# Two chunks that share one FFN by Strassen's products at the end of a streaming encoder layer

## The chip, the core and the metric

The program runs on one core of a Trainium2 chip. Its engines work beside each other, each through its own list of instructions in order: TensorE (PE) multiplies matrices, VectorE (DVE) and ScalarE (ACT) work elementwise on tiles of 128 partitions, GpSimd (POOL) and SyncE (SP) here mostly start DMA transfers. The metric is the device time of one execution in microseconds (us), lower being better.

## The reference

One layer of an encoder over 2048 prompt tokens and 8 x 16 sample tokens, width 1024, FFN width 2816:

```
u = rms_norm(x, norm_mix) @ w_in               # 1024 -> 2564 columns, split among four mixers
x = x + concat(ssd, swa, shortconv, conformer)(u) @ w_out
hf = rms_norm(x, norm_ffn)
x = x + (silu(hf @ w_gate) * (hf @ w_up)) @ w_down
y = rms_norm(x, norm_final)
```

The mixers are a state-space scan in blocks of 64 tokens, attention over a window of 128 keys, a gated convolution over 3 tokens, and a gated convolution over 31 tokens with a layer norm (the conformer). They carry histories from token to token, so the prompt is worked through in order; the final histories and states are outputs too. Everything is float32.

## The kernel before

Activations lie with features on partitions and tokens along the free axis. The 2176 tokens go through in five chunks of 256, 512, 512, 512 (384 of the prompt and the 128 of the sample) and 384 tokens, named c0 to c4 here.

**Products.** Each float32 operand is split into a high part in the matmul's own format (fp32r) and the low part that is left, by one ACT copy and one DVE subtraction (`split`, L177 to L179). `group` (L198) then issues three matmuls for each k-tile of 128: weight high x operand high (L202), weight high x operand low (L203), weight low x operand high (L204), into one PSUM tile `pm`. A projection tile of 1024 inputs so takes 24 matmuls over the chunk's tokens. For each chunk W_in has 21 such tiles, W_out 8, gate and up 22 each, and down (L861) takes 528 matmuls in rounds of 3 or 4 hidden tiles.

**Weights.** `load_w` (L182) starts a DMA of 512 KB on SP into `wr` (3 buffers), copies the high part `wh` on ACT (L192, 2 buffers) and subtracts the low part `wl` on DVE (L164 is the helper `tt`, 2 buffers). These three stand under `high_priority(offset=AHEAD)`, so that the scheduler puts them well ahead of their place in the code. Each weight is loaded and split anew in each chunk.

**A chunk's way.** `proj_in` (L788) makes the W_in tiles, and `after_in` (L368) does what each mixer needs with a tile as it leaves PSUM; the convolutions' inputs go to `raw` tiles (`raw_tiles`, L311, 2 buffers) with their history before them, and `keep_raw` (L345) sends the new histories out by DMA. `mixers` (L747) is a list of generators: attention and scan block by block, the conformer's 31 taps on each of two tiles (`conf_conv`, L363, on DVE, one instruction a tap, into `mix` tiles), and at the end the two norms `end_conf` (L717) and `end_ssd` (L701) and `mix_tile` (L696), which splits the eight results into the operands of W_out. `proj_out` (L799) multiplies them in the order of tiles 4, 5 (short convolution), 2, 3 (attention), 0, 1 (scan), 6, 7 (conformer) and adds x. `norm2` (L825) makes the FFN's operands, `ffn` (L839) returns its 68 units (gate, up and down tiles), `final` (L886) norms and stores.

**The order of the work.** `weave` (L905) puts steps of one list between the units of another. The main loop (from L918) runs, for each chunk c: W_out(c), W_in(c+1), FFN(c). The mixers of c+1 are spread over the first 85% of FFN(c)'s units, so DVE works on them while PE works on the FFN. The order in which instructions stand on each engine is fixed when the program is built. The last four down units of FFN(c3) are put behind W_out(c4). The last chunk has no chunk behind it; its FFN runs alone, at 384 columns a matmul.

## Time and profile before

| | |
|---|---|
| time, median of 3 runs | 2432.99 us (2431.43 to 2434.88) |
| span of the profiled execution | 2430.4 us |
| PE busy | 2386.1 us in 12701 instructions |
| DVE busy | 1648.1 us |
| ACT busy | 919.5 us |
| moved by DMA | 290.78 MB, mean 120 GB/s |

The profiled execution's span of 2430.4 us lies 2.6 us under the median of the runs and 1.0 under the lowest. A row of a profile names a line of the kernel, the engine, the operation, the tile written and the tiles read, and the shape; matmuls on PE overlap, so their rate is read from the distance between two starts, not from the duration of one.

### The profile page before, as it was taken

To read this page: it belongs to the slowest core of one execution; us is meant where nothing else is said; L and a number is where in the kernel's file an instruction comes from. 1 tells how busy PE (TensorE), PEld (TensorE's weight loads), DVE (VectorE), ACT (ScalarE), POOL (GpSimd) and SP (SyncE) were. 2 spreads that over 40 slices of the span, in tenths; PEclk is the share of its full clock that TensorE was granted. 3 is DMA by queue.
4 is the path that set the end of the run, shared out by engine and by line. 5 is a ranking of instruction groups with operands and counts; after the bars stand their busy time and mean duration, and the time that the engine had idled before them with its cause. 6 is when DMAs were issued, how large, how long until landed. Compare 5 with 4: busy or idle time off the path is not lost.

```text
span 2430.4 us, 32788 instructions
## 1 busy us (share of the span) xinstructions
PE 2386.1 (98%) x12701; PEld 2069.4 (85%) x12701; DVE 1648.1 (68%) x2997; ACT 919.5 (38%) x1460; POOL 86.3 (4%) x159
## 2 busy tenths in 40 slices
PE   7999999999999999999999999999999999999998
PEld 7888999888888888877788888889888888999997
DVE  8998998776975546675895455578864545475445
ACT  5544545444333333344333332334332323343332
POOL 1000000000000000001100000000000000000000
PEclk9999999999999999999999999999999999999999
DMA  6433444542222222353422222254322222343332
GB/s 234 135 117 131 158 155 152 199 157 100 90 92 87 87 91 89 137 167 92 135 96 87 87 87 92 91 191 125 112 87 87 90 94 96 133 152 123 131 119 98
DMA packets 106988, 290.78 MB, mean 120 GB/s; under 512 B 10848, under 2 KB 27456, under 8 KB 106832
## 3 DMA queue, kind: packets, MB, share of 16 engines
q1 hardware_dynamic: 102416, 276.34, 34.4%
q0 software_dynamic: 4416, 12.34, 1.6%
q8 instruction: 100, 1.64, 0.3%
q14 instruction: 56, 0.46, 0.1%
HBM read 277.93 MB, written 10.70 MB: 119 GB/s over the span
## 4 chain that ended last, share of the span: by engine, by line
PE 51%; DVE 1%; DMA 1%; issue 0%; ACT 0%; DVEq 0%; ACTq 0%; SPq 0%; POOLq 0%
PE pm L202 16%; PE pm L204 16%; PE pm L203 16%; PE px L231 0%; PE px L213 0%; PE px L640 0%; PE px L622 0%; PE px L650 0%; DMA x<-x 0%; PE px L549 0%; PE px L566 0%; DVE act L167 0%; DMA raw<-gst 0%; PE px L582 0%; DMA y<-x 0%
## 5 line engine op out<-in xcount | busy, mean ns | idle before, releaser
L202 PE MATMUL pm<-act,wh 128*128 128x512 f32 (+2 forms) x2920 | 1056.1, 362 | 3.6 <-ACT act L179 1.4
L204 PE MATMUL pm<-act,wl 128*128 128x512 f32 (+2 forms) x2920 | 1046.5, 358 | 10.8 <-DVE wl L164 10.8
L203 PE MATMUL pm<-act,wh 128*128 128x512 f32 (+2 forms) x2920 | 1045.5, 358 | 0.9 <-DVE act L164 0.9
L192 ACT ACTIVATE wh<-wr 128x1024 fp32r<-128x1024 f32 (+1 forms) x485 | 504.8, 1041 | 1193.8 <-PE pm L203 819.4
L164 DVE TENSOR_TENSOR wl<-wr,wh 128x1024 fp32r<-128x1024 f32 (+1 forms) x485 | 582.5, 1201 | 298.6 <-ACT wh L192 296.7
L204 PEld LDWEIGHTS pm<-act,wl 128*128 128x128 f32 x2920 | 551.8, 189 | 83.6 <-DVE wl L164 13.6
L202 PEld LDWEIGHTS pm<-act,wh 128*128 128x128 f32 x2920 | 551.6, 189 | 79.7 <-ACT wh L192 5.6
L203 PEld LDWEIGHTS pm<-act,wh 128*128 128x128 f32 x2920 | 552.2, 189 | 68.8 <-DVE act L164 1.3
L202 PE MATMUL pm<-h,wh 128*128 128x512 f32 (+2 forms) x880 | 317.7, 362 | 2.0 <-DVE ft L167 1.4
L203 PE MATMUL pm<-h,wh 128*128 128x512 f32 (+2 forms) x880 | 314.3, 357 | 0.0
L204 PE MATMUL pm<-h,wl 128*128 128x512 f32 (+2 forms) x880 | 314.0, 357 | 0.0
L167 DVE SCALAR_TENSOR_TENSOR ft<-ft,pm 128x512 f32<-128x512 f32 (+2 forms) x220 | 132.5, 602 | 166.2 <-PE pm L204 165.3
L164 DVE TENSOR_TENSOR x<-x,pm 128x512 f32<-128x512 f32 (+1 forms) x224 | 137.3, 617 | 134.7 <-PE pm L204 121.2
L167 DVE SCALAR_TENSOR_TENSOR mix<-raw,tabh,mix 128x384 f32<-128x384 f32 (+3 forms) x360 | 199.2, 589 | 1.9
L202 PEld LDWEIGHTS pm<-h,wh 128*128 128x128 f32 x880 | 165.8, 188 | 27.1 <-ACT wh L192 2.7
L203 PEld LDWEIGHTS pm<-h,wh 128*128 128x128 f32 x880 | 165.9, 189 | 20.9 <-issue 0.7
L204 PEld LDWEIGHTS pm<-h,wl 128*128 128x128 f32 x880 | 165.8, 188 | 20.8
L164 DVE TENSOR_TENSOR h<-ft,h 128x512 fp32r<-128x512 f32 (+2 forms) x110 | 66.8, 608 | 0.0
L179 ACT ACTIVATE h<-ft 128x512 fp32r<-128x512 f32 (+2 forms) x110 | 61.1, 555 | 5.3 <-DVE ft L167 4.5
L164 DVE TENSOR_TENSOR ns<-ns,nt 128x512 f32<-128x512 f32 (+2 forms) x91 | 56.9, 625 | 8.9 <-ACT nt L239 7.9
L164 DVE TENSOR_TENSOR act<-act,pm 128x384 f32<-128x384 f32 x56 | 30.9, 552 | 39.6 <-PE pm L204 39.6
L179 ACT ACTIVATE act<-nt 128x512 fp32r<-128x512 f32 (+2 forms) x72 | 40.2, 578 | 45.2 <-DVE nt L167 44.7
(219 smaller groups left out, 1338.6 us busy)
## 6 DMA issues: line engine op xcount, KB each, us to landing
wr<-w_gu SPq DMA_DIRECT2D x220, 512.0 KB, 3.2
wr<-w_in SPq DMA_DIRECT2D x105, 512.0 KB, 3.3
wr<-w_down SPq DMA_DIRECT2D x80, 512.0 KB, 3.4
wr<-w_out SPq DMA_DIRECT2D x40, 512.0 KB, 3.3
wr<-w_down SPq DMA_DIRECT2D x40, 384.0 KB, 3.1
nt<-x SPq DMA_DIRECT2D x48, 256.0 KB, 3.8
x<-x SPq DMA_DIRECT2D x24, 256.0 KB, 5.1
y<-x POOLq DMA_DIRECT2D x24, 256.0 KB, 4.4
```

The costliest lines, as they stand in the source:

```text
L164: return eng.tensor_tensor(out=out, in0=a, in1=b, op=op)
L167: return eng.scalar_tensor_tensor(out=out, in0=a, scalar=s, in1=b, op0=op0, op1=op1)
L179: act.activation(dst[:, 0, :n], src, AF.Copy)
L192: act.activation(hi[:, :n], rv, AF.Copy)
L202: pe.matmul(ps[:, :T], wh, o[:, 0, :T], start=(i == 0), stop=False)
L203: pe.matmul(ps[:, :T], wh, o[:, 1, :T], start=False, stop=False)
L204: mm = pe.matmul(ps[:, :T], wl, o[:, 0, :T], start=False, stop=(i == n - 1))
```

## The change

c0 and c1 go as before. From c2 on the order is another, and c3 and c4 are worked as one block of 896 tokens in the FFN.

- W_in(c3) is made between the first 18 units of FFN(c2), in the order `FIRST`; c3's mixers run up to unit 41 of that FFN, which now has 72 units (`rounds_last`). Then come W_out(c3), units 41 to 43, W_in(c4) merged with units 44 to 48, units 49 to 57, with c4's mixers beside the units from W_in(c4) on, then W_out(c4) and the units 58 to 71.
- x after W_out of c3 and c4 is stored in a DRAM tile `mid`, and the norm's factors are kept in `r2`. `prep` reads `mid` back, scales it, and makes from each pair of k-tiles (i, i + 4) and the two halves of 448 tokens the seven operands of Strassen's scheme, each split into high and low: `11`, `21`, `22`, and four sums `T1` to `T4`.
- Gate and up: two hidden tiles at a time (a quad: 2 halves of the inputs x 2 hidden tiles x 2 halves of the tokens). `quad_w` loads the two tiles' weights, forms four sums and splits seven half-weights; `quad` runs seven products of 12 matmuls over 448 columns instead of eight, into three PSUM tiles, from which ACT copies partial sums between the products. There are 11 quads of gate and 11 of up. The hidden tiles are split and stored in DRAM (`hmem`) by POOL.
- Down: two passes, one for each half of the tokens, all eight output tiles in the eight PSUM banks at once; the operands come back from `hmem`, and `w_down` is read in each pass.
- The split weights of W_in and W_out are kept in DRAM: c0, c1 and c2 each store a third of the 29 tiles (1 MB each, by POOL), and later chunks load high and low together.
- Weight buffers: `w` (high and low in one, 3 buffers) and `fr` (raw, 2 buffers) replace `wr`, `wh` and `wl`.

The core of the diff (the small helpers, `final2`, and the pools' bookkeeping are left out):

```diff
-B = dict(wr=3, wh=2, wl=2, nt=4, b2=4, ut=3, raw=2, mix=4, h=5, ft=1)
+SOON = 120
+B = dict(w=3, fr=2, nt=3, b2=4, ut=3, raw=2, mix=4, act=16, h=5, ft=1)
...
-    def load_w(src, shape, eng=dve):
+    def split_w(raw, n):
+        d = mk(wp, [P, 2, 1024], "w", F32R, bufs=B["w"])
+        act.activation(d[:, 0, :n], raw, AF.Copy)
+        tt(d[:, 1, :n], raw, d[:, 0, :n].bitcast(F32), ALU.subtract)
+        return d
...
+    def load_w(src, shape, key=None, ci=0):
...
-        raw = mk(wp, [P, 1024], "wr", bufs=B["wr"])
-        hi = mk(wp, [P, 1024], "wh", F32R, bufs=B["wh"])
-        lo = mk(wp, [P, 1024], "wl", F32R, bufs=B["wl"])
...
         with tc.high_priority(offset=AHEAD):
-            sync.dma_start(pat(rv), src)
-            act.activation(hi[:, :n], rv, AF.Copy)
-            tt(lo[:, :n], rv, hi[:, :n].bitcast(F32), ALU.subtract, eng)
-        return pat(hi[:, :n]), pat(lo[:, :n])
+            if key in kept:
+                d = mk(wp, [P, 2, 1024], "w", F32R, bufs=B["w"])
+                sync.dma_start(d.bitcast(F32), kept[key])
+            else:
+                raw = mk(wp, [P, 1024], "fr", bufs=B["fr"])
+                sync.dma_start(pat(raw[:, :n]), src)
+                d = split_w(raw[:, :n], n)
+        if key is not None and key not in kept and key % 3 == ci:
+            kept[key] = dp.tile([P, 2, 1024], F32, tag=f"kept{key}", name=f"kept{key}")
+            pool.dma_start(kept[key], d.bitcast(F32))
+        return pat(d[:, 0, :n]), pat(d[:, 1, :n])
...
-    def mixers(c):
+    def mixers(c, early=False):
...
-        if c["i"]:
+        if not early:
             add((short, 1))
...
-        if not c["i"]:
+        if early:
             c["blocks"] = len(st)
             for j, k0, k1 in convs:
                 add((once(lambda j=j, k0=k0, k1=k1: conf_conv(c, j, k0, k1)), 1))
...
+            if m == 0:
+                c["ss"] = mk(np_, [P, TM], "ns", bufs=1)[:, :T]
+            park = c["i"] >= cfg.nfirst
+            x2 = mk(np_, [P, TM], "nt", bufs=B["nt"]) if park else mk(np_, [P, TM], "x2", bufs=8)
             sync.dma_start(x2[:, :T], x[:, m, o:o + T])
-            wh, wl = load_w(w_out[m], [KT, P])
+            wh, wl = load_w(w_out[m], [KT, P], len(W_IN_TILES) + m, c["i"])
...
             tt(x2[:, :T], x2[:, :T], ps[:, :T], ALU.add)
+            if park:
+                pool.dma_start(mid[:, m, o - tail_off:o - tail_off + T], x2[:, :T])
...
+    def stats2(c):
+        o = (c["off"] - tail_off) // P
+        rstd_of(c["ss"], c["T"], D, r2[:, o:o + c["T"] // P])
+        yield
...
-        for ri, n in enumerate(cfg.rounds):
+        for ri, n in enumerate(rounds):
+            end = ri == len(rounds) - 1
...
-                if q == 0:
+                if q == 0 and not (end and lastone):
                     units += pend
                     pend = []
-            pend = [lambda j0=j - n, n=n, m2=m2, f=(ri == len(cfg.rounds) - 1): down(j0, n, m2, f) for m2 in range(4)]
+            pend += [lambda j0=j - n, n=n, m2=m2, f=end: down(j0, n, m2, f) for m2 in range(4)]
...
+    weave(proj_out(c2), (twice(final(c1)), 0, 2), (twice(norm1(c3)), 0, 3))
+    f = ffn(c2)
+    s3 = proj_in(c3, FIRST)
+    units = s3[:3] + merge(s3[3:], f[:18]) + f[18:41]
+    m3 = mixers(c3, True)
+    nb = c3["blocks"]
+    weave(units, (twice(norm2(c2)), 0, 2), (m3[:nb], units.index(s3[8]) + 1, units.index(s3[-1]) + 6),
+          (m3[nb:], units.index(s3[-1]) + 1, len(units) - 1),
+          (twice(norm1_stats(c4)), 20, 35))
+    s4 = proj_in(c4, FIRST)
+    units = proj_out(c3) + f[41:44] + merge(s4, f[44:49]) + f[49:58]
+    m4 = mixers(c4, True)
+    nb = c4["blocks"]
+    weave(units, ([stats2(c3)], 8, 9), (twice(norm1(c4)), 8, 11), (m4[:nb], units.index(s4[8]) + 1, units.index(s4[-1])), (m4[nb:], units.index(s4[-1]) + 1, len(units) - 1))
...
+    def prep():
+        rb = [spread_one(of_blocks(h * N, N)) for h in range(2)]
+        for i in range(4):
+            u = []
+            for k in (i, i + 4):
+                t = g_tile()
+                load_mid(k, t)
+                for h in range(2):
+                    stt(t[:, h], t[:, h], T_("gffn", k), rb[h], ALU.mult, ALU.mult)
+                u.append(t)
+            w = g_tile()
+            b11, b12, b21, b22 = u[0][:, 0], u[0][:, 1], u[1][:, 0], u[1][:, 1]
+            t1, t2 = w[:, 0], w[:, 1]
+            def put(n, src):
+                d = mk(xp if i < 2 else late["xq"], [P, 2, N], "hf", F32R)
+                split(d, src, N)
+                X[n][i] = d
+            put("11", b11)
+            put("21", b21)
+            put("22", b22)
+            tt(t1, b12, b11, ALU.subtract)
+            put("T1", t1)
+            tt(t2, b22, t1, ALU.subtract)
+            put("T2", t2)
+            tt(b12, b22, b12, ALU.subtract)
+            put("T3", b12)
+            tt(t2, b21, t2, ALU.subtract)
+            put("T4", t2)
+            yield
+    def quad_w(j, g):
+        with tc.high_priority(offset=SOON):
+            ra = mk(wp, [P, 1024], "fr", bufs=B["fr"])
+            rb = mk(wp, [P, 1024], "fr", bufs=B["fr"])
+            sync.dma_start(ra.rearrange("p (a b) -> p a b", b=P), w_gu[j, g])
+            sync.dma_start(rb.rearrange("p (a b) -> p a b", b=P), w_gu[j + 1, g])
+            a11, a12, a21, a22 = ra[:, :512], ra[:, 512:], rb[:, :512], rb[:, 512:]
+            s1 = mk(np_, [P, TM], "ft", bufs=B["ft"])[:, :512]
+            da = split_w(ra, 1024)
+            tt(s1, a21, a22, ALU.add)
+            tt(a21, a11, a21, ALU.subtract)
+            tt(a11, s1, a11, ALU.subtract)
+            tt(a12, a12, a11, ALU.subtract)
+            d2 = split_w(ra, 1024)
+            d1 = split_w(s1, 512)
+            dc = split_w(rb, 1024)
...
+    def product(ps, w, xs, first):
+        wh, wl = w
+        n = len(xs)
+        for i, (a, b) in enumerate(xs):
+            pe.matmul(ps[:, :N], wh[:, i], a, start=first and i == 0, stop=False, skip_group_check=True)
+            pe.matmul(ps[:, :N], wh[:, i], b, start=False, stop=False, skip_group_check=True)
+            mm = pe.matmul(ps[:, :N], wl[:, i], a, start=False, stop=(i == n - 1), skip_group_check=True)
+        tail[0] = mm.ins
+    def quad(w):
+        Z, Y, V = (mk(pm, [P, 512], "pm")[:, :N] for _ in range(3))
+        g1, g2 = g_tile(), g_tile()
+        def go(ps, n, first):
+            product(ps, w[n], [(o[:, 0], o[:, 1]) for o in X[XOF[n]]], first)
+        go(Z, 1, True)
+        act.activation(g1[:, 0], Z, AF.Copy)
+        go(Y, 2, True)
+        go(Z, 6, False)
+        act.activation(g1[:, 1], Z, AF.Copy)
+        tt(g1[:, 0], g1[:, 0], Y, ALU.add)
+        go(V, 5, True)
+        act.activation(g2[:, 0], V, AF.Copy)
+        go(Z, 7, False)
+        act.activation(g2[:, 1], Z, AF.Copy)
+        go(V, 3, False)
+        tt(g2[:, 1], g2[:, 1], g2[:, 0], ALU.add)
+        tt(g1[:, 1], g1[:, 1], V, ALU.add)
+        go(Z, 4, False)
+        return g1, g2, Z
...
+    hmem = [dp.tile([P, 2, 2, N], F32, tag=f"hm{j}", name=f"hm{j}") for j in range(cfg.nff)]
+    def gate2(j):
+        g1, g2, Z = quad(quad_w(j, 0))
...
+    def up2(j):
+        g1, g2, Z = quad(quad_w(j, 1))
...
+        stt(t2[:, 1], t2[:, 1], 0.5, g2[:, 1], ALU.mult, ALU.mult)
+        stt(t2[:, 0], t2[:, 0], 0.5, Z, ALU.mult, ALU.mult)
+        for i, t in enumerate((t1, t2)):
+            for h in range(2):
+                d = mk(hp, [P, 2, TM], "h", F32R)[:, :, :N]
+                split(d, t[:, h], N)
+                pool.dma_start(hmem[j + i][:, h], d.bitcast(F32))
+                hs[j + i, h] = d
+    prepared = twice(prep(), 4)
+    weave(proj_out(c4) + f[58:64], ([stats2(c4)], 8, 9), (prepared[:2], 9, 13))
...
+    weave(f[64:], (prepared[2:], 0, 4))
+    units = []
+    for j in range(0, cfg.nff, 2):
+        units += [lambda j=j: gate2(j), lambda j=j: up2(j)]
+    weave(units, (twice(final(c2)), 0, 2))
...
+    def operand(j, h):
+        if j >= cfg.nff - 2:
+            d = hs[j, h]
...
-            side.append(done)
...
+            with tc.high_priority(offset=AHEAD):
+                d = mk(ht, [P, 2, N], "ht", F32R)
+                sync.dma_start(d.bitcast(F32), hmem[j][:, h])
+        return d[:, 0], d[:, 1]
+    def weights(j, mh):
+        with tc.high_priority(offset=AHEAD):
+            raw = mk(wp, [P, 1024], "fr", bufs=B["fr"])
+            sync.dma_start(raw.rearrange("p (a b c) -> p a b c", a=4, b=2), w_down[:, 4 * mh:4 * mh + 4, j:j + 2])
+            d = split_w(raw, 1024)
...
+        acc = [mk(px if m < 4 else pm, [P, 512], "px" if m < 4 else "pm")[:, :N] for m in range(KT)]
+        body, end = (order[:-2], order[-2:]) if h else (order, [])
+        for j in body:
+            ops = [operand(j + i, h) for i in range(2)]
+            for mh in range(2):
+                wh, wl = weights(j, mh)
+                for i in range(4):
+                    product(acc[4 * mh + i], (wh[:, i], wl[:, i]), ops, j == order[0])
+        if not h:
+            for m in range(KT):
+                drain(h, m, acc[m])
...
```

Where the instructions stand, as the built programs have them. First PE in the program before, where the last accumulation ahead of W_out(c4) ends (`pm_3001`, an up tile of FFN(c3)) and W_out(c4)'s first one begins (`pm_3008`; `act_2589` is the short convolution's operand, `act_2946` the first of attention):

```order
L204 MATMUL pm_3001_17927<-act_2472_14597,wl_3000_17923 128x512
L202 MATMUL pm_3008_17965<-act_2589_15353,wh_3006_17960 128x384
L203 MATMUL pm_3008_17965<-act_2589_15353,wh_3006_17960 128x384
L204 MATMUL pm_3008_17965<-act_2589_15353,wl_3007_17961 128x384
L202 MATMUL pm_3008_17965<-act_2590_15356,wh_3006_17960 128x384
L203 MATMUL pm_3008_17965<-act_2590_15356,wh_3006_17960 128x384
L204 MATMUL pm_3008_17965<-act_2590_15356,wl_3007_17961 128x384
L202 MATMUL pm_3008_17965<-act_2946_17596,wh_3006_17960 128x384
L203 MATMUL pm_3008_17965<-act_2946_17596,wh_3006_17960 128x384
```

And the same place in the changed program (`pm_2196`, `pm_2199` and `pm_2203` are W_out(c4)'s first three tiles, `act_2153` and `act_2154` the short convolution's operands, `act_2187` the first of attention, `px_2175` and `px_2184` the spread factors of the mixers' two norms):

```order
L231 MATMUL pm_2203_14908<-act_2153_14616,w_2202_14906 128x384
L232 MATMUL pm_2203_14908<-act_2153_14616,w_2202_14906 128x384
L233 MATMUL pm_2203_14908<-act_2153_14616,w_2202_14906 128x384
L264 MATMUL px_2175_14702<-con_2_85,n8_2164_14654 128x128 x3
L264 MATMUL px_2184_14755<-con_2_85,n8_2172_14686 128x128 x3
L231 MATMUL pm_2203_14908<-act_2154_14619,w_2202_14906 128x384
L232 MATMUL pm_2203_14908<-act_2154_14619,w_2202_14906 128x384
L233 MATMUL pm_2203_14908<-act_2154_14619,w_2202_14906 128x384
L231 MATMUL pm_2196_14842<-act_2187_14767,w_2195_14840 128x384
L231 MATMUL pm_2199_14874<-act_2187_14767,w_2198_14872 128x384
L231 MATMUL pm_2203_14908<-act_2187_14767,w_2202_14906 128x384
L232 MATMUL pm_2196_14842<-act_2187_14767,w_2195_14840 128x384
```

Before, the tiles were made one after the other with no mixer's matmul between; now three are begun on the short convolution's operands alone, and the mixers' norms stand between them. On DVE, the attention's operands before (`act_2946`, `act_2947`), followed by the FFN's own steps (`ft`, `h`, `wl`):

```order
L164 TENSOR_TENSOR act_2935_17524<-xx1_2548_15101,act_2935_17524 128x384
L164 TENSOR_TENSOR act_2946_17596<-q0_2530_14988,act_2946_17596 128x384
L164 TENSOR_TENSOR act_2947_17599<-q1_2535_15021,act_2947_17599 128x384
L167 SCALAR_TENSOR_TENSOR ft_2932_17512<-ft_2932_17512,pm_2939_17533 128x512
L164 TENSOR_TENSOR wl_2950_17604<-wr_2948_17602,wh_2949_17603 128x1024
L164 TENSOR_TENSOR h_2940_17559<-ft_2932_17512,h_2940_17559 128x512
L164 TENSOR_TENSOR wl_2955_17639<-wr_2953_17637,wh_2954_17638 128x1024
```

and in the changed program, where they are `act_2187` and `act_2188`:

```order
L184 SCALAR_TENSOR_TENSOR mix_2132_14423<-ut_2178_14716,mix_2132_14423 128x384
L184 SCALAR_TENSOR_TENSOR xx1_1980_13425<-xx1_1980_13425,tab_1_84,px_2184_14755 128x384
L181 TENSOR_TENSOR act_2177_14711<-mix_2120_14334,act_2177_14711 128x384
L181 TENSOR_TENSOR act_2179_14719<-mix_2132_14423,act_2179_14719 128x384
L181 TENSOR_TENSOR act_2185_14760<-xx0_1975_13386,act_2185_14760 128x384
L181 TENSOR_TENSOR act_2186_14764<-xx1_1980_13425,act_2186_14764 128x384
L181 TENSOR_TENSOR act_2187_14767<-q0_2002_13617,act_2187_14767 128x384
L181 TENSOR_TENSOR act_2188_14770<-q1_2005_13646,act_2188_14770 128x384
L181 TENSOR_TENSOR nt_2194_14838<-nt_2194_14838,pm_2196_14842 128x384
```

Before, FFN steps followed the mixers' last operands; now W_out(c4)'s first addition (`nt_2194`) follows them at once.

More of the change, by code (lines that the diff above doesn't have):

```diff
@@ L225, in rstd_of @@
         stt(r, t, 1.875, r, ALU.add, ALU.mult)
+    def rstd_of(sq, T, n, r=None):
+        nb = T // P
+        v, r_, t = (mk(cp, [P, 8], "n8", bufs=9)[:, :nb] for _ in range(3))
+        r = r_ if r is None else r
+        pc = mk(px, [P, 512], "px")
+        for b in range(nb):
+            pe.matmul(pc[:, b:b + 1], sq[:, b * P:(b + 1) * P], ones[:, 0:1], start=True, stop=True)
+        newton(v, r, t, pc[:, :nb], n)
         return r
@@ new lines, in of_blocks, with spread_one, load_mid @@
+    def of_blocks(o, n_):
+        out, at = [], 0
+        while at < n_:
+            b, t0 = divmod(o + at, P)
+            n = min(P - t0, n_ - at)
+            out.append((r2[:, b:b + 1], t0, at, n))
+            at += n
+        return out
+    def spread_one(r):
+        pr = mk(px, [P, 512], "px")
+        for col, t0, at, n in r:
+            pe.matmul(pr[:, at:at + n], bc(col, [P, P]), ident[:, t0:t0 + n], start=True, stop=True)
+        return pr[:, :N]
+    def load_mid(k, t):
+        sync.dma_start(t, mid[:, k].rearrange("p (h n) -> p h n", h=2))
```

183 lines of the change are left out of this document (130 added, 53 removed).

## The prediction

> **What bounds the kernel now.** I read the page first, then the busy time by stages, then single rows.
>
> ```profile
> span 2430.4 us, 32788 instructions
> PE 2386.1 (98%) x12701; PEld 2069.4 (85%) x12701; DVE 1648.1 (68%) x2997; ACT 919.5 (38%) x1460; POOL 86.3 (4%) x159
> PEclk9999999999999999999999999999999999999999
> ```
>
> TensorE (PE) is busy 98% of the span at full clock, so the number and length of its matmuls set the time, and the other engines matter only where they make it wait. The busy time by stages, one row each, shows where that is:
>
> ```profile
> core 0: us, PE busy (x) PEld busy (x) DVE busy (x) ACT busy (x) POOL busy (x), PEclk, DMA share, GB/s
> ...
> 40.00:360.00 320.00, 318.51 (x2173) 286.85 (x2173) 296.74 (x632) 164.73 (x301) 14.18 (x24) 1.00 0.43 143
> ...
> 1020.00:1200.00 180.00, 169.42 (x739) 137.83 (x738) 130.78 (x251) 66.25 (x99) 22.19 (x33) 0.98 0.48 142
> ...
> 1600.00:1980.00 380.00, 379.11 (x1866) 324.98 (x1865) 247.09 (x409) 137.03 (x216) 17.38 (x31) 1.00 0.35 113
> ...
> 2040.00:2400.00 360.00, 358.65 (x1989) 346.45 (x1988) 195.33 (x279) 119.12 (x158) 4.32 (x8) 1.00 0.39 130
> 2400.00:2430.40 30.40, 18.39 (x103) 17.43 (x101) 18.61 (x40) 6.96 (x13) 0.00 (x0) 0.84 0.18 65
> ```
>
> Three things stand there. The last chunk's FFN (2040 to 2400) runs on PE without a gap while VectorE (DVE) is half idle: that is the work the change shortens. The projection of the sample chunk (1020 to 1200) leaves PE idle for 10.6 us. And while the mixers run (1600 to 1980) DVE works 65% of the time, beside an FFN that covers it.
>
> The time of one matmul is the distance between two starts, since the listed durations overlap:
>
> ```profile
> start us, us, engine line op out<-in xcount [idle before <-releaser]
> ...
> 999.65 0.39 PE L202 MATMUL pm<-h,wh 128*128 128x512 f32 x1
> 999.88 0.39 PE L203 MATMUL pm<-h,wh 128*128 128x512 f32 x1
> ...
> 1000.56 0.39 PE L203 MATMUL pm<-h,wh 128*128 128x512 f32 x1
> ...
> 2198.72 0.33 PE L202 MATMUL pm<-h,wh 128*128 128x384 f32 x1
> 2198.89 0.33 PE L203 MATMUL pm<-h,wh 128*128 128x384 f32 x1
> ...
> 2199.76 0.33 PE L202 MATMUL pm<-act,wh 128*128 128x384 f32 x1
> ```
>
> From 999.65 to 1000.56 are four steps: 227 ns for 512 columns. From 2198.72 to 2199.76 are six: 173 ns for 384. No matmul of 448 columns runs before; halfway between the two is 200 ns, and I take it, because 448 is halfway between the widths.
>
> **The change part by part.**
>
> *Strassen, the gain.* Before, chunks 3 and 4 take 1056 gate and up matmuls and 528 down matmuls each: 1584 x (0.227 + 0.173) = 633.6 us. After, 22 quads of 7 products of 12 matmuls are 1848, and down is 1056, all of 448 columns: 2904 x 0.200 = 580.8 us. The difference is -52.8 us, all on the path, since PE is the bound there. It is the 264 matmuls saved; merging the chunks alone saves nothing. The Trainium skill ("TensorE: Matmul & The Clock Gate", "Wait — 56ns, not 53.3ns?") gives N/2.4 + 2.5 ns, an estimate of 189 ns for 448 columns and of -50 us for the 264; the rows above, 11 ns longer at both widths, decide.
>
> *The sample chunk's wait.* Its first projection ran alone on PE before. These are PE's waits from 1020 to 1200 and DVE's from 1100 to 1200, and PE's stretch just behind the last of them:
>
> ```profile
> PE pm L204 <- DVE wl L164: 10.3, 6, 3.7
> ```
>
> ```profile
> DVE raw L315 <- DMA o_xc_s<-raw: 12.6, 3, 4.8
> DVE raw L171 <- DMA raw<-gst: 5.4, 2, 3.5
> ```
>
> ```profile
> 1161.00:1164.00 3.00, 3.00 (x8) 2.34 (x8) 3.00 (x8) 0.00 (x0) 0.00 (x0) 0.50 0.23 22
> ```
>
> DVE stood on two `raw` buffers that DMAs had not let go, the low part of the next weight (`wl`) queued behind it on DVE, and PE waited 10.3 us for that. In the change all of this chunk's W_in tiles come from DRAM already split (each of the chunks before kept a third), so no `wl` stands behind `raw`, and 18 units of chunk 2's FFN lie between the tiles. I take -10 us, with 0 (the wait only moves to the tiles' readers) and -14 (the stretch at half clock goes too) as ends.
>
> *Chunk 4's mixers before W_out(4), the largest cost.* Before, they were done by 85% of chunk 3's FFN. Now they begin beside W_in(4), and the FFN left beside them is nine units. I count from the last W_in tile (a0's accumulation) on. PE then has 144 matmuls of 512 columns, 66 of 384 (18 of them W_out on the two short-convolution tiles) and a few small ones until it needs the attention's two tiles: 144 x 0.227 + 66 x 0.173 + 3 = 47.1 us. DVE's durations, from the chunk before's mixers:
>
> ```profile
> L164 DVE TENSOR_TENSOR wl<-wr,wh 128x1024 fp32r<-128x1024 f32 x70 | 85.6, 1224 | 47.8 <-ACT wh L192 47.7
> L167 DVE SCALAR_TENSOR_TENSOR mix<-raw,tabh,mix 128x384 f32<-128x384 f32 x60 | 34.9, 613 | 0.6
> ...
> ```
>
> ```profile
> 1754.56 2.73 DVE L167 SCALAR_TENSOR_TENSOR mix<-raw,tabh,mix 128x384 f32<-128x384 f32 x5
> 1757.21 0.68 DVE L167 SCALAR_TENSOR_TENSOR ft<-ft,pm 128x512 f32<-128x512 f32 x1
> 1757.81 1.22 DVE L164 TENSOR_TENSOR wl<-wr,wh 128x1024 fp32r<-128x1024 f32 x1
> 1758.94 0.69 DVE L164 TENSOR_TENSOR b<-b,xC 128x512 f32<-128x512 f32 x1
> 1759.54 0.69 DVE L164 TENSOR_TENSOR h<-ft,h 128x512 fp32r<-128x512 f32 x1
> 1760.15 2.21 DVE L167 SCALAR_TENSOR_TENSOR mix<-raw,tabh,mix 128x384 f32<-128x384 f32 x4
> ```
>
> Starts again: five taps, of 613 ns each by duration, take 2.73, so a tap is (2.73 - 0.61) / 4 = 0.53 us; a weight's low part 1.13; an addition over 512 columns 0.60. In the new order DVE has, up to the sum `ut` of the two convolutions, 60 taps (31.8 us), five low parts of 1024 and four of 256 (5.7 + 1.3), ten additions into x2 (6.0), four 512-wide FFN steps (2.5) and fifteen others, nine over 384 columns (5 us): 52.8 us. Behind `ut` come the two norms (22 tiny steps at some 0.2 us) and fifteen full ones at 0.5 to 0.6, 13 us. So the attention's tiles stand at 65.9 us, and PE, with 47.1 us of work, waits 18.8. The chain between the engines (mean on PE, square on ACT, spread on PE) adds an estimated 1.5, and a wait this long ends in a stretch at half clock like the one above, which costs 1.5. I take +21 us; the ends are 12 (DVE's steps a tenth shorter, 59.3 - 47.1, and no chain or half clock on top) and 28 (a tenth longer, 72.5 - 47.1, and both on top). The Trainium skill (same page, "Why this matters for your kernels") warns of PE gaps of over some 3 us, after which the clock is halved; the row with 0.50 agrees, and by the page this wait would cost about as much as I added.
>
> *Entry to the quads.* `prep` must read x back from DRAM, scale it and make seven operands of each of four pairs of k-tiles. From the spreading of the norm to the first quad PE has 216 matmuls of 512 columns, 49.6 us. DVE in that stretch has 28 low parts, 12 differences and 4 plain ones over 448 (44 x 0.53), 16 scalings (0.60), eleven low parts of weights (3 x 1.13, 4 x 0.87, 4 x 0.60), and 18 FFN and x2 steps (0.60), two more for the first quad's weights: 54.4 us to the first quad's weights, and 66.2 to its last ones, which PE wants at 59.2. So +5 to +7, and the reloads over three `g` buffers, 3.2 us each by the row below, show in part: +9, ends 4 and 15.
>
> ```profile
> wr<-w_gu SPq DMA_DIRECT2D x220, 512.0 KB, 3.2
> ```
>
> *Inside the quads.* A quad is 84 x 0.200 = 16.8 us on PE. DVE has 3.5 low parts of 1024 (4.0), four sums of weights (2.4), three sums of products (1.6) and the gate's or up's steps (2.1 to 4.3): 10 to 12.5 us. It fits, so +2, ends 0 and 25 (a rival).
>
> *Smaller terms.* Chunk 3's mixers share DVE with more FFN than before: 5 us for blocks that wait (0 to 9). From the last quad to down, four operands must be split first: +3 (1 to 6). Storing split weights (30 MB by GpSimd's queue) and reloading lies beside PE work at 120 GB/s of traffic: 0, and if the cover were gone a 1 MB load is some 6 us. Two `fr` buffers in place of three `wr`: +2 (-2 to 25, a rival). The tail stays as it was.
>
> Sum: 2430.4 - 52.8 - 10 + 21 + 9 + 2 + 5 + 3 + 2 = 2409.6 us against the profiled execution. The median of the runs shown, 2432.99, is 2.6 above its span; 2409.6 + 2.6 = 2412 us.
>
> **The rivals.**
>
> *More of the gain stays.* DVE is busy 68% overall and could be ahead at both boundaries; then W_out(4) costs 12 and the entry 4, and the half-clock stretch goes too: 2430.4 + 2.6 - 52.8 - 14 + 12 + 4 + 5 = 2387 us. Against it: DVE cannot begin the 60 taps before their tile is there, and they are half of its sum.
>
> *Slower: two raw buffers starve the first chunk.* The weight loads of chunk 0's 256-token FFN, seen by the low parts in one stretch, and what a load goes through:
>
> ```profile
> 240.00:360.00 120.00, 79.28 (x279) 53.32 (x279) 43.32 (x36) 1.00 0.46 153
> ...
> ```
>
> ```profile
> L192 ACT ACTIVATE wh<-wr 128x1024 fp32r<-128x1024 f32 (+1 forms) x485 | 504.8, 1041 | 1193.8 <-PE pm L203 819.4
> ```
>
> 36 weights in 120 us, one each 3.33 us. A raw buffer is taken for the DMA (3.2), the high part (1.04) and the low part (1.22): 5.5 us, so two give one each 2.75 us. It decides from 6.7 us a cycle on, 1.2 us of queueing on a DVE that is 93% busy in that stage. At 8 us the weights come each 4.0 us, and some 75 of them lose 0.67: +50, 2412 - 2 + 50 = 2460 us. For it: DVE's load there. Against it: w has three buffers, so a late load has a whole weight of slack, and chunk 1 takes a third of its projection's weights already split.
>
> *The quads run at the pace of their chain.* Z passes from PE to ACT and back between products, with three `fr`, `w` and `g` hand-overs a quad. If each quad loses 1.1 us, 22 of them lose 25: 2412 - 2 + 25 = 2435 us, no change that can be told. For it: 12.5 of 16.8 us on DVE in strict order. Against it: a copy of 448 columns is covered by the product between (12 x 0.200 = 2.4 us).
>
> That the change doesn't do what it says is out: in the program's order the 1848 and 1056 matmuls of 448 columns stand there.
>
> **How the numbers follow.** Chances: the forecast 0.60, more of the gain 0.20, quads at their chain's pace 0.09, two raw buffers 0.11. The forecast's own range is 2399 to 2425: its terms' ends lie some 7, 8, 6 and 5 us from the values taken, which as independent errors make 13. The range takes in the first rival, with 3 us for a pitch of 199 instead of 200 ns on 2904 matmuls, and the quads' rival: 2384 to 2436. A measurement of this kernel can tell about 0.2% (4.9 us) from no change: below 2428 is faster. Faster 0.83 (the first two, and a third of the quads' case, where a quad loses less), the same 0.05 (most of what is left of that case), slower 0.12 (the raw buffers, and the quads' bad end).
>
> **What would show it.** Right: matmuls of 448 columns starting 200 ns apart; PE waiting some 17 us before W_out(4), first for the convolutions' sum and then for the attention's tiles, and 5 to 10 us around the first quad; no wait for `raw` in chunk 3. Wrong: PE waiting in small pieces all over chunk 0 for low parts, or in each quad for `w`, or a pitch other than 200 ns.

## The result, and the profile after

The changed kernel takes 2468.18 us (2461.09 to 2471.18, 4 runs) against 2432.64 for the kernel before on the same chip: 1.0136 times as long, 95% interval 1.0116 to 1.0155. It is slower where faster was forecast. The profiled execution has a span of 2459.3 us, 28.9 more than before. It is the fastest of the four, 7 us under their median; what follows accounts for this one.

The page of the changed kernel, its span, the engines and the clock by slices:

```profile
span 2459.3 us, 32394 instructions
PE 2367.5 (96%) x12443; PEld 2052.3 (83%) x12443; DVE 1589.3 (65%) x2997; ACT 876.7 (36%) x1461; POOL 130.8 (5%) x240
...
PEclk9999999999999999999999999999889999999998
DMA  7657445576422222466443136643533323338663
```

PE has 258 matmuls fewer, but is busy only 96% of a longer span, and the clock now falls below full in the slices around 1700 to 1850 us. A longer span with less work means waits. PE's waits, by what it waited for (total, times, longest):

```profile
PE pm L231 <- DVE x L181: 15.0, 7, 9.2
PE px L257 <- DVE ns L181: 12.9, 2, 10.8
PE px L264 <- DVE n L184: 9.3, 3, 4.4
PE pm L231 <- DMA w<-kept: 7.0, 7, 2.0
PE pm L231 <- ACT act L196: 6.9, 3, 3.0
PE pm L233 <- DVE w L181: 5.1, 8, 0.8
PE pm L231 <- ACT hf L196: 4.5, 2, 4.3
```

The second line is the lead-in, which the kernel before has too. To see where the time went I counted the projection and FFN matmuls (PE's `pm` ones and, in the down passes, those into `px`), whose order is the same in both kernels up to the end of W_out(c2), and compared when the same one starts; the column of excess is the stretch less N/2.4 + 13.3 ns for each of them (N columns; a line through the means of the kernel before, 119.9, 173.4 and 227.1 ns at 256, 384 and 512) and less the mixers' small matmuls.

| stretch | before | after | excess before | excess after |
|---|---|---|---|---|
| to the 600th (W_in(c0) and four tiles of W_in(c1)) | 117.2 us | 135.3 us | 15 | 34 |
| to the 2784th (FFN(c0) done) | 460.5 | 477.5 | 11 | 10 |
| to the 5256th (W_out(c2) done) | 1058.9 | 1084.7 | 8 | 17 |
| from there to the last matmul | 1363.4 long | 1366.1 long | 32 | 78 |

So 25.8 us are lost in chunks 0 to 2, which the forecast had at +2; and from there on the 52.8 us gained are spent on 46 us more excess and 10 us more in the mixers' small matmuls, which the forecast had at +30 together.

The first stretch, 17 to 117 us, one row each of before and after (busy time and count of PE first, then the other engines, clock, DMA share, GB/s):

```profile
17.00:117.00 100.00, 98.65 (x698) 89.56 (x699) 93.08 (x219) 58.89 (x115) 5.85 (x10) 1.00 0.51 173
```

```profile
17.00:117.00 100.00, 85.22 (x607) 78.01 (x607) 76.50 (x180) 52.17 (x107) 8.47 (x17) 0.98 0.72 255
```

In the same 100 us PE gets 91 matmuls fewer through, DVE and ACT idle more too, and the DMA traffic is half as high again. The DMA issues of that stretch, first the weight loads before, then loads and stores after (KB each, us to landing), and what ACT waited for there after:

```profile
wr<-w_in SPq DMA_DIRECT2D x24, 512.0 KB, 3.3
```

```profile
fr<-w_in SPq DMA_DIRECT2D x21, 512.0 KB, 4.4
kept<-w POOLq DMA_DIRECT2D x7, 1024.0 KB, 6.4
```

```profile
ACT w L201 <- DMA fr<-w_in: 18.9, 9, 4.1
```

A weight lands 4.4 us after its issue, not 3.3 as before, and ACT waits 18.9 us for weights; before, no wait of ACT for a weight's load stands on its list there.

Chunk 4's wait came, with about the size that was forecast. The stretches around it and around the first quad:

```profile
1696.00:1712.00 16.00, 6.75 (x19) 4.69 (x19) 16.00 (x29) 3.17 (x4) 0.00 (x0) 0.68 0.30 99
1724.00:1744.00 20.00, 15.48 (x68) 13.99 (x67) 11.80 (x40) 5.53 (x12) 0.06 (x1) 0.66 0.13 53
1832.00:1844.00 12.00, 6.18 (x15) 4.32 (x15) 11.36 (x20) 3.99 (x8) 0.00 (x0) 0.61 0.25 84
1853.00:2222.00 369.00, 368.17 (x1827) 341.38 (x1826) 253.15 (x361) 164.47 (x249) 32.68 (x48) 1.00 0.35 118
2230.00:2430.00 200.00, 200.00 (x1002) 187.42 (x1001) 62.80 (x65) 49.33 (x53) 2.44 (x4) 1.00 0.68 223
```

In the first row DVE is busy for all of the 16 us and PE for 6.75, with the clock down at 0.68. The last two rows are the quads and the down passes: PE is busy throughout. Strassen's part does what it was built for.

### The profile page after: what moved, and what is told of

Same layout as the page of the kernel before. It is cut to its first block, busy times and chain, and to the rows that moved or that the text cites. A ratio compares the mean times of both kernels' runs of the same rounds, so it can differ in the third digit from the quotient of the medians.

```text
span 2459.3 us, 32394 instructions
## 1 busy us (share of the span) xinstructions
PE 2367.5 (96%) x12443; PEld 2052.3 (83%) x12443; DVE 1589.3 (65%) x2997; ACT 876.7 (36%) x1461; POOL 130.8 (5%) x240
## 4 chain that ended last, share of the span: by engine, by line
PE 44%; issue 6%; DVE 3%; DMA 2%; ACT 0%; POOL 0%; DVEq 0%; SPq 0%; POOLq 0%; ACTq 0%
PE pm L1102 6%; PE pm L1103 6%; PE pm L1104 6%; PE pm L231 6%; PE pm L232 6%; PE pm L233 6%; PE px L1103 1%; PE px L1102 1%; PE px L1104 1%; DMA nt<-x 1%; DVE w L181 1%; DVE x L184 0%; DMA o_xc_s<-raw 0%; DMA act<-kc 0%; PE px L655 0%
## 5 line engine op out<-in xcount | busy, mean ns | idle before, releaser
L231 PE MATMUL pm<-act,w 128*128 128x512 f32 (+2 forms) x2216 | 804.2, 364 | 16.6 <-DMA w<-kept 7.0
L233 PE MATMUL pm<-act,w 128*128 128x512 f32 (+2 forms) x2216 | 796.8, 360 | 5.2 <-DVE w L181 5.1
L232 PE MATMUL pm<-act,w 128*128 128x512 f32 (+2 forms) x2216 | 795.8, 359 | 1.4 <-DVE act L181 1.4
L201 ACT ACTIVATE w<-fr 128x1024 fp32r<-128x1024 f32 (+3 forms) x375 | 388.3, 1036 | 892.9 <-PE pm L233 524.1
L181 DVE TENSOR_TENSOR w<-fr,w 128x1024 fp32r<-128x1024 f32 (+3 forms) x375 | 448.4, 1196 | 288.3 <-ACT w L201 287.0
L231 PEld LDWEIGHTS pm<-act,w 128*128 128x128 f32 x2216 | 420.2, 190 | 85.2 <-issue 9.4
L233 PEld LDWEIGHTS pm<-act,w 128*128 128x128 f32 x2216 | 420.3, 190 | 64.6 <-DVE w L181 7.5
L232 PEld LDWEIGHTS pm<-act,w 128*128 128x128 f32 x2216 | 420.6, 190 | 59.4 <-DVE act L181 2.3
L1102 PE MATMUL pm<-hf,w 128*128 128x448 f32 x616 | 225.6, 366 | 0.8 <-ACT g L1116 0.6
L1103 PE MATMUL pm<-hf,w 128*128 128x448 f32 x616 | 224.8, 365 | 0.0
L1104 PE MATMUL pm<-hf,w 128*128 128x448 f32 x616 | 223.8, 363 | 0.0
L231 PE MATMUL pm<-h,w 128*128 128x512 f32 (+1 forms) x528 | 192.3, 365 | 19.6 <-DVE x L181 12.9
L232 PE MATMUL pm<-h,w 128*128 128x512 f32 (+1 forms) x528 | 189.2, 359 | 0.0
L233 PE MATMUL pm<-h,w 128*128 128x512 f32 (+1 forms) x528 | 188.3, 357 | 0.0
L181 DVE TENSOR_TENSOR x<-x,pm 128x512 f32<-128x512 f32 (+2 forms) x184 | 107.6, 600 | 67.4 <-PE pm L233 55.1
L231 PEld LDWEIGHTS pm<-h,w 128*128 128x128 f32 x528 | 100.3, 190 | 41.1 <-issue 12.3
L184 DVE SCALAR_TENSOR_TENSOR ft<-ft,pm 128x512 f32<-128x512 f32 (+1 forms) x132 | 78.7, 596 | 84.2 <-PE pm L233 67.2
L1102 PEld LDWEIGHTS pm<-hf,w 128*128 128x128 f32 x616 | 115.6, 188 | 10.6 <-ACT g L1116 1.0
L1104 PEld LDWEIGHTS pm<-hf,w 128*128 128x128 f32 x616 | 115.7, 188 | 9.4
L1103 PEld LDWEIGHTS pm<-hf,w 128*128 128x128 f32 x616 | 115.7, 188 | 8.2
L233 PEld LDWEIGHTS pm<-h,w 128*128 128x128 f32 x528 | 100.4, 190 | 15.2
```

The costliest lines, as they stand in the source:

```text
L181: return eng.tensor_tensor(out=out, in0=a, in1=b, op=op)
L184: return eng.scalar_tensor_tensor(out=out, in0=a, scalar=s, in1=b, op0=op0, op1=op1)
L201: act.activation(d[:, 0, :n], raw, AF.Copy)
L231: pe.matmul(ps[:, :T], wh, o[:, 0, :T], start=(i == 0), stop=False)
L232: pe.matmul(ps[:, :T], wh, o[:, 1, :T], start=False, stop=False)
L233: mm = pe.matmul(ps[:, :T], wl, o[:, 0, :T], start=False, stop=(i == n - 1))
```

## The experiments

Each was run against the kernel before on the same chip; "excess" is as above. Where a row tells of a matmul by its number, it is the count above.

**What slows the first chunks: the stores or the buffers.** Theory A is the traffic of the 1 MB stores, theory B, the forecast's rival, the two raw buffers. The first run stores nothing, the second stores later, the third is the kernel before with two raw buffers.

```diff
-        if key is not None and key not in kept and key % 3 == ci:
+        if False:
```

> The changed kernel with no split weights kept in DRAM: every chunk loads and splits W_in and W_out anew, all else as in the changed kernel. Theory A (the 1 MB stores of split weights are what slows the first chunk's projection: they share the DMA engines with the weight loads): the 600th projection matmul starts within 4 us of the kernel before (117 us) instead of 18 us later, and the whole falls to 2440 to 2455 us, since W_in of the later chunks is split on VectorE again. Theory B (two raw weight buffers are what slows it): the 600th starts at 131 us or later, and the whole stays at 2462 us or more.

```diff
-        if key is not None and key not in kept and key % 3 == ci:
+        if key is not None and key not in kept and ci in (1, 2) and key % 2 == ci - 1:
```

> The changed kernel, but the first chunk keeps no split weights; the second and the third chunk keep one half each, so that chunks 3 and 4 still load all of them split. Theory A (stores): the first stage's 18 us go, the stage around the second chunk's projection loses up to 4 us more, whole 2446 to 2456 us. Theory B (two raw buffers): the first stage stays 14 us or more behind the kernel before, whole 2462 us or more.

```diff
-B = dict(wr=3, wh=2, wl=2, ...
+B = dict(wr=2, wh=2, wl=2, ...
```

> The kernel before with two instead of three raw weight buffers, nothing else. Theory A (stores are the cause in the first chunk): within 5 us of the kernel before, 2433 to 2438 us. Theory B (two raw buffers are the cause): the 600th projection matmul starts 12 us or more later than 117 us, whole 2447 us or more.

Measured: 2452.4 us without stores (ratio 1.0064, 1.0044 to 1.0084), 2458.5 with later stores (1.0102, 1.0082 to 1.0121), 2448.2 for the kernel before with two raw buffers (1.0044, 1.0029 to 1.0059). The 600th matmul starts at 121.8, 121.0 and 122.2 us (before 117.2, changed 135.3). The rows of the stretch without stores and of the kernel before with two raw buffers:

```profile
17.00:117.00 100.00, 95.14 (x680) 85.55 (x679) 88.95 (x209) 58.24 (x116) 4.42 (x10) 1.00 0.53 173
```

```profile
17.00:117.00 100.00, 95.44 (x677) 86.42 (x677) 89.98 (x210) 57.86 (x115) 3.87 (x10) 1.00 0.51 167
```

They are alike: two raw buffers alone cost 5 us here, and the stores the other 14. Neither theory is the whole, but A has three quarters. Three figures lie outside what was expected: the 600th matmul of the first run by 0.6 us, the whole of the second by 2.5, and the whole of the third, which stands where theory B had it. In the kernel before, two raw buffers cost more than this stretch shows: 10 us by the 5256th matmul, and 12 in the median of the whole. Up to the 5256th matmul the run without stores is 5.5 us behind the kernel before, the changed kernel 25.8. The difference of 20 holds the stores and also the reloads in chunks 1 and 2, where PE waits 4 us for `w<-kept`. The kept weights are worth something later: without them the second half of the profiled execution is 16 us longer, probably because W_in and W_out of chunks 3 and 4 are split on DVE again. By the medians, which differ by 16 us and not by the 4 of the profiled executions, it would be some 5 us, if the first half gains the same 20 in them. Storing later (the second run) saves half of the 25.8: the 5256th starts at 1072.8.

**Traffic alone.** To see whether a store hurts by its traffic or by holding one of the three `w` buffers, the same 1 MB is written from a constant tile, after a small copy that waits for the split weight. No chunk loads kept weights here.

```diff
-            pool.dma_start(kept[key], d.bitcast(F32))
+            dm = dp.tile([P, 4, 512], F32, tag=f"kept{key}", name=f"kept{key}")
+            one = mk(cp, [P, 8], "n8", bufs=9)
+            pool.tensor_copy(one[:, :1], d[:, 1, :1].bitcast(F32))
+            pool.dma_start(dm, cn[:, :512].unsqueeze(1).to_broadcast([P, 4, 512]))
```

> The changed kernel, but at each place where split weights are stored the same 1 MB is written from a constant tile instead, started when the split weight is ready, and no chunk loads kept weights. So the traffic is there and no weight buffer is held by a store. Theory A (traffic): the 600th projection matmul starts at 130 us or later, as in the changed kernel (135). Theory B (a store holds one of three weight buffers for its 6 us): it starts at 125 us or earlier, as with no stores (122).

Measured: the 600th starts at 160.1 us, later still than in the changed kernel.

```profile
17.00:117.00 100.00, 73.94 (x512) 68.08 (x512) 62.04 (x142) 43.10 (x82) 15.41 (x26) 0.93 0.89 329
```

```profile
kept<-con POOLq DMA_DIRECT2D x15, 1024.0 KB, 9.4
fr<-w_in SPq DMA_DIRECT2D x19, 512.0 KB, 6.1
```

Weights land after 6.1 us here. But the test is much stronger than wanted. The store itself has no tie to the small copy, and GpSimd issues six in a row right behind the first copy, where the second copy comes only at 50.42 us:

```profile
14.68 4.40 POOL L224 DMA_DIRECT2D kept<-con  x6
```

So 15 stores lie in the stretch where the changed kernel has 7, and each takes 9.4 us, not 6.4. That shows that traffic alone, at twice the stores, delays the loads; it does not show that the real stores' traffic makes up the 14 us, nor that holding the buffer adds nothing.

**More cover for chunk 4's mixers.** Cover is PE work beside which the mixers' work on DVE is hidden.

```diff
-    units = s3[:3] + merge(s3[3:], f[:18]) + f[18:41]
+    units = s3[:3] + merge(s3[3:], f[:18]) + f[18:36]
...
-    units = proj_out(c3) + f[41:44] + merge(s4, f[44:49]) + f[49:58]
+    units = proj_out(c3) + f[36:39] + merge(s4, f[39:44]) + f[44:58]
```

> The changed kernel with five FFN units of the third chunk moved from beside chunk 3's mixers to beside chunk 4's mixers (27 us of TensorE work). If the wait ahead of the last W_out (some 23 us with the half clock) is VectorE being 19 us behind TensorE: it falls to under 5 us, whole 2443 to 2450 us. Rival (the wait only moves to chunk 3's W_out, or it is a DMA that is late): whole 2460 us or more.

Measured: 2463.97 us (1.0118, 1.0103 to 1.0133), 4 less than the changed kernel. The excess from the end of W_in(4) to the end of W_out(4) falls from 23 to 9 us, so DVE's lateness made most of it, though less fell away than was expected (to under 5 us); but chunk 3's stretch has 11 us more, most of it here:

```profile
PE px L655 <- ACT b L644: 7.3, 1, 7.3
```

That is a block of chunk 3's attention that PE reached before its softmax was done. The rival holds, in the whole too: cover taken from one chunk's mixers is missed at the other's.

**What Strassen itself brings.** Each quad with eight plain products; the operands `T1` to `T4` and the sums of weights are not made.

```diff
-        go(Z, 1, True)
-        go(Y, 2, True)
-        go(Z, 6, False)
...
+        def go(ps, t, h):
+            for q in range(2):
+                product(ps, w[t][q], [(o[:, 0], o[:, 1]) for o in X[f"{q + 1}{h + 1}"]], q == 0)
```

> The changed kernel with eight plain products in place of Strassen's seven in each quad: the operands are only the four blocks (16 split tiles in place of 28, no sums), a quad is 96 matmuls of 448 columns, all else as in the changed kernel. Theory A (Strassen gives its matmuls nearly whole, and costs only at the entry): the stretch from the first 448-column matmul to the last of the quads is 53 us longer, the wait ahead of the first quad falls from 17 to under 8 us, whole 2498 to 2515 us. Theory B (the quads wait for VectorE and ScalarE and give the gain back): the quads' stretch is less than 40 us longer, whole under 2490 us.

Measured: 2508.8 us (1.0301, 1.0275 to 1.0327), 41 more than with seven products. From the first to the last matmul of 448 columns it takes 642.2 us against 590.3: 51.9, forecast 52.8. The excess ahead of the first quad falls from 17.3 to 6.4. Theory A holds: the products give their whole gain in the quads, and pay 11 us at the entry.

**Why 512 columns take 229 ns.** In the middle chunks matmuls of the changed kernel start 229.1 ns apart, those of before 227.1 (means over 5029 and 6603). Two runs of the kernel before, one with both parts of a weight in one tile, one with the operands' pools allocated from the other end of the memory (`side="right"` on `ap`, `hp` and `np_`):

```diff
-        hi = mk(wp, [P, 1024], "wh", F32R, bufs=B["wh"])
-        lo = mk(wp, [P, 1024], "wl", F32R, bufs=B["wl"])
+        d = mk(wp, [P, 2, 1024], "w", F32R, bufs=B["wh"])
+        hi, lo = d[:, 0], d[:, 1]
```

> The kernel before, with the high and low part of a weight in one tile of 8 KB a partition, two buffers, instead of two tiles of 4 KB. The 512-column matmuls of the changed kernel start 229 ns apart in the middle chunks, those of the kernel before 227. If the combined weight tile is the cause, it is 229 ns here and the whole some 8 to 12 us over the kernel before; if not, 227 ns and no change.

> The kernel before, with the pools of the operands, hidden tiles and norms allocated from the other end of the on-chip memory, as in the changed kernel. If the place of the operands is the cause of the longer distance between matmuls, it is 229 ns here and the whole some 8 to 12 us over the kernel before; if not, 227 ns and no change.

Measured: 2438.1 us and 227.1 ns with one tile, that is nothing; 2474.7 us (one run) and 233.3 ns with the pools at the other end, 37 us more for a mere change of place. An estimate from the distances in the table at the end, times the matmuls of each width, gives 39. Steps of that run:

```profile
900.00 0.39 PE L203 MATMUL pm<-act,wh 128*128 128x512 f32 x1
900.23 0.40 PE L204 MATMUL pm<-act,wl 128*128 128x512 f32 x1
900.46 0.39 PE L202 MATMUL pm<-act,wh 128*128 128x512 f32 x1
900.70 0.40 PE L203 MATMUL pm<-act,wh 128*128 128x512 f32 x1
900.93 0.39 PE L204 MATMUL pm<-act,wl 128*128 128x512 f32 x1
901.16 0.40 PE L202 MATMUL pm<-act,wh 128*128 128x512 f32 x1
```

Five steps in 1.16 us, where five of before take 1.135. Then the kernel before with unused tiles that move everything, or the operands alone:

```diff
+    pad = mk(cp, [P, 56], "pad")
     tb = mk(cp, [P, NTAB], "tab")
```

> The kernel before with one unused tile of 224 bytes a partition ahead of all others, so that the operands and weights of every projection matmul start at multiples of 256 bytes instead of 32 bytes past one. Theory (the start addresses set the distance between matmuls, as the two layouts with 227 and 233 ns suggest): the distance at 512 columns changes by 2 ns or more, and the whole by 12 us or more, either way. Rival (only the place of operands against weights counts, which is the same as before): 227 ns and 2433 to 2440 us.

```diff
+    pad2 = sp.tile([P, 32], F32, tag="pad2", name="pad2")
     ap = ctx.enter_context(tc.tile_pool(name="ap", bufs=16))
```

> As the run before it, with the operands another 128 bytes on: weights at multiples of 256 bytes, operands 128 past one. Theory (addresses against 64 bytes count): as the run before it. Rival (operands against weights counts): a distance other than in the run before it by 2 ns or more at 512 columns.

Measured: 2435.6 us and 227.1 ns (0.9997, 0.9988 to 1.0006) with everything moved to a multiple of 256 bytes; 2472.2 us (one run) and 232.5 ns with the operands another 128 bytes on. So the shared address made no difference in the places tried, the operand's place against the weight's did, as the rivals in both expectations had it.

**Putting it together.** First, only chunk 3 stores split weights (for chunk 4), and five units go from beside W_in(3) to chunk 4's mixers:

```diff
-        if key is not None and key not in kept and key % 3 == ci:
+        if key is not None and key not in kept and ci == 3:
...
-    units = s3[:3] + merge(s3[3:], f[:18]) + f[18:41]
+    units = s3[:3] + merge(s3[3:], f[:13]) + f[13:36]
```

> The changed kernel, but only chunk 3 keeps split weights (for chunk 4 alone), and five FFN units of the third chunk go from beside W_in(3) (13 instead of 18 there) to beside chunk 4's mixers; chunk 3's own mixers have as many units as in the changed kernel. If the stores are what slows the first three chunks, the second projection's end stands within 7 us of the kernel before (1065 us instead of 1085); if chunk 4's mixers only lack cover, the wait ahead of the last W_out falls from 23 to under 10 us; chunk 3's projection may wait 5 to 12 us more for its raw tiles. Together 2430 to 2446 us. Rival (the waits ahead of W_out(3) and W_out(4) are one budget of cover, and only move): 2448 us or more.

Measured: 2446.55 us (1.0032, 1.0018 to 1.0046). The 5256th matmul starts at 1063.9, chunk 4's excess is 8, and chunk 3's stretch rises from 22 to 38: two parts as forecast, the third dearer; the whole lies between the forecast's range and the rival's. Then the same with two unused tiles of 32 bytes, which put operands and weights at the same place against 256 bytes:

> The kernel of the run with stores by chunk 3 only, with two unused tiles of 32 bytes, so that operands and weights start at multiples of 64 bytes (192 past a multiple of 256). If addresses against 64 bytes set the distance: under 227 ns at 512 columns and under 200 at 448, whole under 2436 us. If only operands against weights counts: 227 and 200 ns as in the kernel before, whole 2434 to 2440 us. If neither: 229 ns, 2446 us.

Measured: 227.1 ns at 512 columns but 202.9 at 448 (changed kernel 200.9 and, for a third of them, 202.6), 2447.83 us (1.0048, 1.0032 to 1.0065), no different from the run without the tiles. The distance at 512 is what "only operands against weights" had, the one at 448 and the whole are not. What is won at 512 columns (2.0 ns each, some 10 us, an estimate from the means) is lost again at 448 (1.5 ns, 4 us) and 256 (2.7 ns, 6 us). In its projection of chunk 3 DVE stands like this:

```profile
1073.04 0.16 DVE L189 SCALAR_TENSOR_TENSOR n<-n,n 128x4 f32<-128x4 f32 x1
1078.72 0.17 DVE L353 COPY raw<-hx 128x3 f32<-128x3 f32 x1 [5.52 <-DMA o_xc_s<-raw]
1078.80 0.15 DVE L186 TENSOR_TENSOR n<-n,n 128x4 f32<-128x4 f32 x1
```

The copy into `raw` waits 5.5 us for the DMA that still reads the tile, and the steps of the norm (`n`) for chunk 2's FFN stand on DVE behind it. PE's waits there:

```profile
PE px L528 <- ACT ut L519: 6.2, 1, 6.2
PE px L269 <- DVE n L189: 5.5, 1, 5.5
```

Four tiles that use `raw` were made in a row; so another order, in which only the last two still follow each other:

```diff
-    s3 = proj_in(c3, FIRST)
+    s3 = proj_in(c3, ("k", "v", "q0", "B", "q1", "C", "dt", "x0", "x1") + FIRST[9:])
```

> The kernel of the run before (stores by chunk 3 only, tiles at 64 bytes), with the first nine W_in tiles of chunk 3 in another order: three that need no raw tile come first, and the four that need one are parted by others. If the two raw tiles are what VectorE waits for there, with the norm's steps behind it: PE's two waits of 5.7 and 6.3 us in the projection of chunk 3 fall to under 2 us each, whole 2430 to 2440 us. Rival (VectorE is simply behind there, whatever it waits for): both stay within 2 us, whole 2445 us or more.

Measured: 2426.93 us (0.9964, 0.9952 to 0.9976), below the range forecast. In that projection PE now waits for one thing:

```profile
PE pm L238 <- DVE w L186: 2.2, 1, 2.2
```

Last, two units moved from chunk 3's mixers to the entry:

```diff
-    units = s3[:3] + merge(s3[3:], f[:13]) + f[13:36]
+    units = s3[:3] + merge(s3[3:], f[:13]) + f[13:34]
...
-    weave(proj_out(c4) + f[58:64], ([stats2(c4)], 8, 9), (prepared[:2], 9, 13))
+    weave(proj_out(c4) + f[56:64], ([stats2(c4)], 8, 9), (prepared[:2], 9, 13))
```

> As the run before, and two FFN units of the third chunk (11 us of TensorE work) moved from beside chunk 3's mixers to behind W_out(4), ahead of the first quad. If chunk 3's mixers have cover to spare and the entry lacks it: the wait ahead of the first quad falls from 17 to 8 us or less with none in its place, whole 6 to 10 us under the run before, 2422 to 2434 us. Rival (it is one budget and only moves): within 3 us of the run before.

Measured: 2424.42 us (0.9953, 0.9941 to 0.9966), within 3 us of the run before. The excess ahead of the first quad falls only from 19.0 to 13.5, and chunk 3's rises from 20.7 to 25.4: the rival holds, it is one budget. The page of this version:

```profile
span 2422.6 us, 32577 instructions
PE 2358.4 (97%) x12443; PEld 2052.6 (85%) x12443; DVE 1656.9 (68%) x3056; ACT 932.7 (38%) x1520; POOL 130.4 (5%) x242
```

By the two ratios it beats the kernel before by 0.5% and the changed one by 1.8%.

## Why the prediction was wrong

Its sum, term by term, in us:

| term | forecast | measured | shown by |
|---|---|---|---|
| Strassen's products | -52.8 | -51.9 | seven against eight products |
| storing and reloading split weights, chunks 0 to 2 | 0 | +20 | no stores: 5256th matmul at 1064.4 for 1084.7 |
| two raw buffers | +2 | +5 | no stores: 5.5 us still behind there (the new places of the tiles are in it) |
| chunk 3's projection | -10 | -3 | excess 11.5 for 14.2 |
| chunk 3's mixers | +5 | +9 | excess and small matmuls |
| chunk 4's mixers ahead of W_out(4) | +21 | +22 | 19 of excess, the rest small matmuls; cover moved: falls by 14 |
| W_out(4)'s own waits | 0 | +4 | excess of its last 174 matmuls |
| entry to the quads | +9 | +16 | eight products: falls by 11 |
| inside the quads | +2 | +5 | 202 ns a matmul |
| last quad to down | +3 | 0 | the first down matmul starts 0.4 us after the last of the quads |
| the tail | 0 | +3 | 18.3 us from the last down matmul to the end, 14.8 before |

*The step that failed* is the one of the smaller terms: "Storing split weights (30 MB by GpSimd's queue) and reloading lies beside PE work at 120 GB/s of traffic: 0". The runs show +20 in its place. The mean over the span was the wrong row. In the stretch where the first stores lie the traffic before was 173 GB/s and a weight's load 3.3 us long; with two raw buffers and no stores ACT already waits 11.5 us for loads there, and with stores, where the load takes 4.4 us, 18.9. The profiled execution's span missed the forecast by 50 us (2459.3 for 2409.6), and this term is 20 of them, the largest but not the whole: the entry and chunk 3's projection are 7 each, and 2 to 4 each come from most of the others. Without the stores the kernel still takes 2452 us, outside the range.

The forecast's rival named the first chunk and its raw buffers and gave it 0.11, but placed the loss in chunk 0's FFN and put it down to queueing on DVE. The excess did not grow in that FFN (10 for 11); it grew in W_in ahead of it, where DVE idled for a quarter of the time and ACT waited for the DMA. The sign given for it, PE waiting in small pieces for low parts, came (`w L181` in the list of PE's waits: 8 times, 5.1 us), but is the smaller part.

*Chunk 3's projection* failed as a place: the wait for `raw` was seen, but it did not go, as the forecast's signs had it: DVE waits 12.3 us for `raw<-gst` in that chunk and 4.2 for `o_xc_s<-raw`. The claim that none of this chunk's low parts stands behind it was right, but other work does. The norm of chunk 2's FFN now stands there (4.4 us at one place), and the order `FIRST` makes four tiles with `raw` in a row. With the tiles parted the profiled execution is 14.4 us shorter, 12.0 of it excess and 2.8 small matmuls in this stretch: the waits and the half clock behind them. The medians differ by 21; the runs of the version without it reach from 2440 to 2450, so the rest is not told apart.

*The entry* was right in kind and short in size: DVE's sum against PE's gave +5 to +7, and it was 16. PE's waits from 1780 to 1853 add up to 10.3 us; the rest is in stretches at a lower clock (0.61 in the row of 1832 to 1844). The reloads over three `g` buffers, which the forecast named, show as a wait of DVE of only 0.6 us. What in the chain set the 16 is shown only as far as the run with eight products goes: 11 of the 16 fall away with the sums and their splits.

*Chunk 4's wait* was forecast to within some 2 us, from the order of the instructions and the durations of before (the steps listed up to `ut` add up to 52.3 us, not 52.8, which changes nothing). Its place was right in part only. PE was to wait first for the convolutions' sum; the longest wait, 9.2 us up to about 1707, came earlier, at a down unit whose PSUM tile was free only when DVE, in its order, got to the addition behind the taps:

```profile
1701.27 4.86 DVE L184 SCALAR_TENSOR_TENSOR mix<-raw,tabh,mix 128x384 f32<-128x384 f32 x9
1706.03 0.69 DVE L181 TENSOR_TENSOR x<-x,pm 128x512 f32<-128x512 f32 x1
```

*The pitch*, the distance between two starts, was forecast at 200 ns for 448 columns; it is 200.9 or 202.6 by where the operands lie. That the pitch of the other widths would change was not in the sum: 512 columns lose 2.0 ns each and 256 win 2.8, some +10 and -6 us by an estimate from the means, spread over the rows of the table. The Trainium skill ("TensorE: Matmul & The Clock Gate", "Wait — 56ns, not 53.3ns?") gives N/2.4 + 2.5 ns, an estimate of 189 ns for 448 columns; no layout here came near, the shortest mean step at 512 columns being 227 ns where it gives 216.

What stays open: how much of the stores' cost is the buffer they hold; what sets chunk 3's remaining excess of some 20 us, which is spread over many blocks; and what makes the other three runs of the changed kernel 5 to 10 us longer than the profiled one.

## What to carry to other kernels

Price a new transfer in the stretch where it will run, by the landing time of the loads it runs beside and the buffers that hide them, not by the mean traffic. A product that saves matmuls is only half the change: count what must be ready before its first one, and whose cover that takes; when two late stages share one cover, moving it between them gains little, and removing a wait (here by the order of four tiles) gains more. And when pools are moved, compare the distance between matmuls before anything else.

## What the runs showed of the hardware

In these runs the distance between two matmuls goes with where the moving operand lies against the stationary one, modulo 256 bytes in a partition (addresses from the built programs, the same for all matmuls of a width unless noted):

| operand's start less weight's | 256 columns | 384 | 448 | 512 |
|---|---|---|---|---|
| 0 (kernel before, the same moved by 224 bytes, and the version at multiples of 64 bytes) | 119.9 ns | 173.4 | 202.9 | 227.1 |
| 64 (changed kernel) | 117.1 | 173.3 | 200.9 | 229.1 |
| 128 (operands another 128 bytes on) | 118.9 | 176.0 | | 232.5 |
| 192 (pools at the other end) | 115.3 | 176.5 | | 233.3 |

At 512 columns the best and the worst differ by 2.7%, at 256 by 4% the other way. Only four differences were tried, with weights loaded for every matmul. At 448 columns the stage counts as well: in the changed kernel a third of these matmuls, all in the quads, have a difference of 0 and start 202.6 ns apart; those at 64 start 201.8 ns apart in the quads and 200.0 in the down passes, which makes the 200.9. Why the place counts was not looked into.
